# Row products and convolution taps from GpSimd and ScalarE to VectorE, and another start for a ring of split weights

## The chip, the cores and the metric

The kernel runs on one core of a Trainium2 chip. The metric is the device time in microseconds (us) of one execution, and lower is better. The core's engines run side by side: TensorE (PE in the rows) multiplies matrices, VectorE (DVE), ScalarE (ACT) and GpSimd (POOL) work on elements, SyncE (SP) issues most transfers. Each engine takes its instructions in the order in which they stand in its queue.

## What is computed

Two transformer blocks of two layers each, one after the other, in f32 on 512 positions of 1024 features. The change lies in the second block and at the seam to it. Of the reference, this is what the changed lines compute:

```python
return rmsnorm(x, final_norm_w)                    # end of the first block
...
for l in range(DEPTH):                             # second block
    h = rmsnorm_2(x, norm_mix_g[l]) * (1.0 + sc1) + sh1
    u = h @ w_in[l]
    ...                                            # four mixers on slices of u
    y_conv = conformer_conv(cu, conv_w[l], conv_b[l], conv_ln_g[l], conv_ln_b[l])
    mix = jnp.concatenate([y_fox, y_pool, y_ret, y_conv], axis=-1)
    x = x + g1 * (mix @ w_out[l])
    h = rmsnorm_2(x, norm_ffn_g[l]) * (1.0 + sc2) + sh2
    f = (jax.nn.silu(h @ ffn_w1[l]) * (h @ ffn_w3[l])) @ ffn_w2[l]
    x = x + g2 * f

def conformer_conv(u, conv_w, conv_b, ln_g, ln_b):
    a, gate = jnp.split(u, 2, axis=-1)
    h = a * jax.nn.sigmoid(gate)
    h = lax.conv_general_dilated(                  # 31 taps, one filter per channel
        h, conv_w[:, None, :], window_strides=(1,), padding=[(CONV_WIDTH - 1, 0)],
        dimension_numbers=('NWC', 'WIO', 'NWC'), feature_group_count=CONV_CH) + conv_b
    return jax.nn.silu(layernorm(h, ln_g, ln_b))
```

The convolution has 256 channels, which are two tiles of 128 channels x 512 positions.

## The kernel before

Features lie on the 128 partitions, positions along the free axis: x is eight tiles of 128x512. Every f32 product of matrices is made of three products of rounded parts: `mm3` (L290 to L292) multiplies the high part of a weight with the high part of the input, the same with the input's low part, and the weight's low part with the input's high part. Inputs are split into `hx[0]` (high) and `hx[1]` (low) by `modulate`: a product `hmod` on VectorE (L522), the high part on ScalarE (L523) and the low part on VectorE (L524), in halves of 256 positions.

The class `Weights` loads each weight into one of four `wraw` buffers and splits it: `whi` by a copy on ScalarE (L204), `wlo = wraw - whi` by a subtraction on VectorE (L205), for a few entries of the plan on GpSimd in two halves. `parts` says where the two results lie. In the mixers that is the pool `split`, with two buffers. While `extra` is set, which is so in the feed-forward, a pool of its own with two more pairs joins, and `n_ring` alternates between the two, beginning with `extra`. The memory of `extra` was the mixers' before, and becomes free as the mixers end.

At the end of the first block, `w_out_phase` with l = 1 makes the last norm twice: into `hx`, from which the second block's mixers start, and into the tiles `x2`, which carry x on. `Norm.rows` turns a column of 512 factors into `R1`, a 128x512 tile in PSUM with the same row on all partitions, ScalarE copies it to SBUF (`R1s`), and GpSimd multiplies the eight tiles of `x2` with it (L724).

In the mixers (class `Mix`) the projection `w_in` goes through TensorE slice by slice, while the parts of the mixers that are ready run beside it. `conv_in` makes, for each of its two tiles, the gated input `hp` and hands a generator of 31 taps to a list from which a few are drawn after each weight. A tap adds 512 columns of `hp`, shifted by one more, times a column of `cw`, to the sum `cacc`. For tile 0 every tap is one instruction on VectorE (L2105). For tile 1, taps 1 to 30 are two: ScalarE makes the product `tap` (L2108), GpSimd adds it (L2109). `conv_out` then sums over both tiles on GpSimd (`both`, L2138) and normalises.

The order of the instructions on each engine comes from a scheduler that places them by its own estimate of their times; `issue_after` is a hint to it that one is to come behind another. So an edit in one place moves instructions in others too.

In the feed-forward, weights 0 and 2 are from w1, 1 and 3 from w3 for the first two slices, which are made with `mm3` into `dps`. After them a scheme with fewer products follows: it needs eight sums of `hx` parts (`xa`, L1496), four more (L1499 to L1505), and the matmuls into `sd`, `sfc`, `sy` and others (L1522 to L1524).

Of the kernel before, what the change touches and what calls it, by code (L numbers as in the profile page):

```python
# [9 lines left out]
F32 = mybir.dt.float32  # L10
# [3 lines left out]
AF = mybir.ActivationFunctionType  # L14
OP = mybir.AluOpType
# [24 lines left out]
KORD = (4, 5, 6, 7, 8, 9, 10, 11, 0, 1, 2, 3)  # L40
LEAD = (0.22, 0.35)
MLEAD = 0.45
PTAP = (0, 31)
CONVW = 2
OORD = (2, 0, 3, 6, 7, 4, 5, 1)
TRATE = (3, 3)
# [10 lines left out]
def parts(x, bits):  # L57

    out = []
    for _ in range(3):  # L60
        e = math.floor(math.log2(abs(x)))
        c = math.floor(x / 2.0 ** (e - bits + 1)) * 2.0 ** (e - bits + 1)
        out.append(c)
        x -= c
    return out + [x]


TURN = parts(2 * math.pi, 9)
PI_LO = 3.1415925

# [5 lines left out]
class Weights:  # L76
# [45 lines left out]

    def parts(self):

        self.n_ring = (self.n_ring + 1) % 2 if self.extra else 0
        pool, k = (self.extra, {"bufs": 2}) if self.n_ring else (self.split, {})
        return [pool.tile([128, KD * 128], F32R, tag=x, name=x, **k) for x in ("whi", "wlo")]

    def free(self, n):
# [153 lines left out]
class Kern:  # L283
# [340 lines left out]
    def w_out_phase(self, l, s):  # L624
        tc, nc, a = self.tc, self.nc, self.a
        V, A = nc.vector, nc.scalar
# [20 lines left out]
        m = self.mod[l]  # L647
        acc = xp.tile([128, 512], F32, name="accx")
        acc2 = xp.tile([128, 512], F32, name="accc")
        if l:  # L650
            x2, fw = self.B2.x, self.vecs[:, 64:72]
# [33 lines left out]
        for ct in range(7):  # L685
            px = self.pt("d", "wox")
            pc = self.pt("pt" if ct else "d", "woc") if l == 0 else None
            for p in range(2):
                w = self.W.next()
# [6 lines left out]
        w = [self.W.next(2 - i) for i in range(2)]  # L696
# [21 lines left out]
        if l:  # L718
            R1 = self.pt("pt", "R1")
            nm.rows(R1, 0, 4, 2, 0)  # L720
            R1s = self.tmp.tile([128, 512], F32, tag="hmod", name="R1s")
            A.activation(R1s, R1, AF.Copy)
            for k in range(8):
                nc.gpsimd.tensor_tensor(x2[:, k, :], x2[:, k, :], R1s, op=OP.mult)  # L724


class Attn:
# [921 lines left out]
class Mix:  # L1649
# [442 lines left out]
    def conv_in(self, t):  # L2092
        nc = self.nc
        V, A, tc = nc.vector, nc.scalar, self.K.tc
        hp, acc = self.hp[t], self.cacc[t]

        def taps():
            for i in range(31):
                src, w = hp[:, 2 + i:514 + i], self.cw[:, t, i:i + 1]
                s, v = self.K.W.last  # L2100
                with tc.issue_after(s), tc.issue_after(v):
                    if i == 0:
                        V.tensor_scalar(acc, src, w, self.col(2, t), op0=OP.mult, op1=OP.add)
                    elif i >= PTAP[t]:
                        V.scalar_tensor_tensor(acc, src, w, acc, op0=OP.mult, op1=OP.add)  # L2105
                    else:
                        m = self.K.tmp.tile([128, 512], F32, tag="hmod", name="tap")
                        A.activation(m, src, AF.Copy, scale=w)  # L2108
                        nc.gpsimd.tensor_tensor(acc, acc, m, op=OP.add)  # L2109
                yield  # L2110

        def f(ps):
            nc.gpsimd.memset(hp[:, 0:32], 0.0)
            nc.vector.scalar_tensor_tensor(hp[:, 32:], self.th, 1.0, ps, op0=OP.add, op1=OP.mult)
            self.taps.append((taps(), TRATE[t]))
        return f
# [305 lines left out]
```

## Time and profile before

| | |
|---|---|
| median of three runs | 2502.6 us (2501.32 to 2503.1) |
| the profiled execution | 2502.77 us, span 2501.0 us |
| busy: TensorE, VectorE | 2359.8 us (94%), 1922.1 us (77%) |
| busy: ScalarE, GpSimd | 1365.9 us (55%), 222.2 us (9%) |
| first mixers and their feed-forward entry | from 1282 to 1552 us of the span |
| second mixers and their feed-forward entry | from 1895 to 2162 us of the span |

Times in the rows are microseconds from the start of the span. A row of a timeline is one instruction or several alike that follow each other: start, busy time, engine, line, operation, what is written and read, the count, and in brackets how long the engine sat idle before and what ended that. Instructions of one engine overlap a little, so a row's time is more than its distance to the next. In the rows the tile x2 is called x, and R1 is R. Lines are those of the kernel before; in the changed kernel the same lines stand one to seven lower.

### The profile page before, as it was taken

The page shows a single profiled execution, that of the slowest core. Times are in us where ns is not written, and L with a number is a line of the kernel's source. Part 1 is how long each engine was busy: PE and PEld are TensorE (multiplying, and loading weights), DVE is VectorE, ACT ScalarE, POOL GpSimd, SP SyncE. Part 2 cuts the span into 40 slices and gives each one's busy share as a digit, 9 for nine tenths or more (in the row PEclk, how much of TensorE's full clock was granted, in tenths as well). Part 3 has the DMA queues.
Part 4 walks back from the last instruction along what each step waited for, and adds up shares of the span by engine and source line. Part 5 has one row for each costly group of instructions (what it writes and reads, how often), then busy time and mean ns, then how long its engine had stood idle before and what let it go on. Part 6 is the DMA issues. An engine that isn't in the chain of part 4 may idle for free. (4 is left out here: it accounts for less than half of the span.)

```text
span 2501.0 us, 37762 instructions
## 1 busy us (share of the span) xinstructions
PE 2359.8 (94%) x14392; PEld 2034.3 (81%) x14392; DVE 1922.1 (77%) x3269; ACT 1365.9 (55%) x2656; POOL 222.2 (9%) x206
## 2 busy tenths in 40 slices
PE   7899999999998999999987998999999899899998
PEld 3788888888887788888775778989897578899897
DVE  5778777888356888888579868999767985967675
ACT  4566555668345654578546555535355655545453
POOL 0110000000020000000035201000002510100000
PEclk9999999999999999999989999999999899999999
DMA  6113323223331146532422122676332212242422
GB/s 258 48 55 93 97 95 103 88 85 125 131 96 50 45 150 217 190 120 64 133 73 65 54 66 78 232 247 213 116 101 76 66 56 68 85 132 72 128 71 72
DMA packets 87749, 269.67 MB, mean 108 GB/s; under 512 B 12048, under 2 KB 22544, under 8 KB 87184
## 3 DMA queue, kind: packets, MB, share of 16 engines
q1 hardware_dynamic: 78240, 232.79, 28.9%
q10 hardware_dynamic: 6912, 25.17, 2.9%
q0 software_dynamic: 2416, 9.31, 1.0%
q8 instruction: 113, 1.85, 0.3%
q14 instruction: 68, 0.56, 0.1%
HBM read 255.82 MB, written 11.40 MB: 107 GB/s over the span
## 5 line engine op out<-in xcount | busy, mean ns | idle before, releaser
L290 PE MATMUL dps<-hx,whi 128*128 128x512 f32 (+1 forms) x1040 | 417.0, 401 | 16.1 <-ACT q L1747 5.0
L292 PE MATMUL dps<-hx,wlo 128*128 128x512 f32 (+1 forms) x1040 | 404.4, 389 | 9.4 <-DVE wlo L205 8.3
L291 PE MATMUL dps<-hx,whi 128*128 128x512 f32 (+1 forms) x1040 | 405.2, 390 | 2.8 <-DVE hx L524 1.7
L204 ACT ACTIVATE whi<-wraw 128x1024 fp32r<-128x1024 f32 (+2 forms) x202 | 194.0, 964 | 263.6 <-issue 84.3
L205 DVE TENSOR_TENSOR wlo<-wraw,whi 128x1024 fp32r<-128x1024 f32 (+1 forms) x182 | 221.8, 1219 | 82.0 <-ACT whi L204 80.4
L290 PEld LDWEIGHTS dps<-hx,whi 128*128 128x128 f32 x1040 | 203.4, 196 | 46.1 <-DVE t L1770 6.4
L292 PEld LDWEIGHTS dps<-hx,wlo 128*128 128x128 f32 x1040 | 203.0, 195 | 46.1 <-DVE wlo L205 9.1
L1165 ACT ACTIVATE ph<-PT 128x512 fp32r<-128x512 f32 (+1 forms) x280 | 152.9, 559 | 135.7 <-PE PT L1160 132.4
L291 PEld LDWEIGHTS dps<-hx,whi 128*128 128x128 f32 x1040 | 203.3, 195 | 27.6 <-DVE hx L524 3.3
L1166 DVE TENSOR_TENSOR pl<-PT,ph 128x512 fp32r<-128x512 f32 (+1 forms) x280 | 175.3, 642 | 44.6 <-ACT ph L1165 42.4
L162 ACT ACTIVATE whi<-wraw 128x512 fp32r<-128x512 f32 x200 | 119.5, 625 | 131.7 <-PE spt L1523 42.4
L1148 PE MATMUL Y<-ph,vt 128*128 128x256 f32 (+1 forms) x592 | 161.1, 282 | 6.6 <-ACT ph L1165 2.8
L1160 PE MATMUL PT<-ident,P 128*128 128x128 f32 x1024 | 160.0, 276 | 5.9 <-DVE pl L1166 4.0
L1149 PE MATMUL Y<-pl,vt 128*128 128x256 f32 (+1 forms) x592 | 162.5, 290 | 2.7 <-DVE pl L1166 2.6
L290 PE MATMUL w2p<-g,whi 128*128 128x512 f32 (+1 forms) x364 | 140.5, 386 | 0.0
L291 PE MATMUL w2p<-g,whi 128*128 128x512 f32 (+1 forms) x364 | 140.4, 386 | 0.0
L292 PE MATMUL w2p<-g,wlo 128*128 128x512 f32 (+1 forms) x364 | 140.4, 386 | 0.0
L1160 PEld LDWEIGHTS PT<-ident,P 128*128 128x128 f32 x1024 | 118.8, 141 | 23.2 <-DVE pl L1166 9.7
L1148 PEld LDWEIGHTS Y<-ph,vt 128*128 128x128 f32 x592 | 111.6, 189 | 28.2 <-ACT ph L1165 19.0
L1099 PE MATMUL S<-kt,qt 128*128 128x256 f32 (+2 forms) x576 | 126.7, 328 | 1.7 <-DVE nm L1117 0.9
L1149 PEld LDWEIGHTS Y<-pl,vt 128*128 128x128 f32 x592 | 111.8, 189 | 13.7 <-DVE pl L1166 6.1
L1118 ACT ACTIVATE P<-P,nm 128x512 f32<-128x512 f32 (+1 forms) x128 | 94.9, 742 | 47.5 <-DVE nm L1117 46.0
(477 smaller groups left out, 6546.2 us busy)
## 6 DMA issues: line engine op xcount, KB each, us to landing
wraw<-ffn_w SPq DMA_DIRECT2D x120, 512.0 KB, 4.4
wraw<-w_in SPq DMA_DIRECT2D x112, 512.0 KB, 3.5
adaw<-ada_wt SPq DMA_DIRECT2D x80, 512.0 KB, 4.0
adab<-ada_wt ACTq DMA_DIRECT2D x48, 512.0 KB, 5.2
wraw<-w_out SPq DMA_DIRECT2D x32, 384.0 KB, 3.1
aw<-ada_w SPq DMA_DIRECT2D x16, 512.0 KB, 10.2
wraw<-w_out SPq DMA_DIRECT2D x16, 512.0 KB, 3.5
bias<-bias_b SPq DMA_DIRECT2D x16, 384.0 KB, 3.7
```

Source lines behind the costliest of these rows:

```text
L162: self.nc.scalar.activation(hi[:, j * w:j * w + w], x, AF.Copy)
L204: s = self.nc.scalar.activation(hi[:, q], t[:, q], AF.Copy)
L205: v = E.tensor_tensor(lo[:, q], t[:, q], fr(hi[:, q]), op=OP.subtract)
L290: mm(ps, hi, xh, start=start, stop=False)
L291: mm(ps, hi, xl, start=False, stop=False)
L292: self.mm_last = mm(ps, lo, xh, start=False, stop=stop).ins
L1099: mm(S[:, so:so + n], Q[:, j, qc], Kt[:, i, ko:ko + n], start=i == 0, stop=i == 1)
L1148: mm(o, v, ph[:, co:co + w], start=b == 0 and n == 0, stop=False, skip_group_check=True)
L1149: mm(o, v, pl[:, co:co + w], start=False, stop=b == len(banks) - 1 and n == len(items) - 1, skip_group_check=True)
L1160: nc.tensor.transpose(pst[:, col:col + 128], ps[t][:, pc:pc + 128], K.ident)
L1165: A.activation(ph[:, :col], pst[:, :col], AF.Copy)
L1166: V.tensor_tensor(pl[:, :col], pst[:, :col], fr(ph[:, :col]), op=OP.subtract)
```

## The change

Three edits. In `w_out_phase`, VectorE multiplies the eight tiles of `x2` with `R1` in PSUM, and ScalarE's copy goes. In `conv_in`, all taps of both tiles are one instruction on VectorE; 30 taps per layer move. In `Weights.parts`, the ring of the feed-forward counts four and takes the pool `split` for the first two pairs and `extra` for the next two, where it took them in turn.

```diff
-PTAP = (0, 31)
...
     def parts(self):
 
-        self.n_ring = (self.n_ring + 1) % 2 if self.extra else 0
-        pool, k = (self.extra, {"bufs": 2}) if self.n_ring else (self.split, {})
+        pool, k = (self.extra, {"bufs": 2}) if self.extra and self.n_ring > 1 else (self.split, {})
+        self.n_ring = (self.n_ring + 1) % 4 if self.extra else 0
         return [pool.tile([128, KD * 128], F32R, tag=x, name=x, **k) for x in ("whi", "wlo")]
...
             R1 = self.pt("pt", "R1")
             nm.rows(R1, 0, 4, 2, 0)
-            R1s = self.tmp.tile([128, 512], F32, tag="hmod", name="R1s")
-            A.activation(R1s, R1, AF.Copy)
             for k in range(8):
-                nc.gpsimd.tensor_tensor(x2[:, k, :], x2[:, k, :], R1s, op=OP.mult)
+                V.tensor_tensor(x2[:, k, :], x2[:, k, :], R1, op=OP.mult)
...
                     if i == 0:
                         V.tensor_scalar(acc, src, w, self.col(2, t), op0=OP.mult, op1=OP.add)
-                    elif i >= PTAP[t]:
+                    else:
                         V.scalar_tensor_tensor(acc, src, w, acc, op0=OP.mult, op1=OP.add)
-                    else:
-                        m = self.K.tmp.tile([128, 512], F32, tag="hmod", name="tap")
-                        A.activation(m, src, AF.Copy, scale=w)
-                        nc.gpsimd.tensor_tensor(acc, acc, m, op=OP.add)
```

VectorE's queue at the start of the first mixer, before (hx_79 is the low part of the input, ck a constant of the mixers, cw the filters):

```order
L524 SCALAR_TENSOR_TENSOR hx_79<-hmod,mod_9634,hx_78 128x256 x2
L522 TENSOR_TENSOR hmod<-x,rrow 128x256 x2
L1845 CAST ck<-ones 64x512
L524 SCALAR_TENSOR_TENSOR hx_79<-hmod,mod_9634,hx_78 128x256 x2
L205 TENSOR_TENSOR wlo<-wraw,whi 128x1024
L1664 TENSOR_SCALAR cw<-cw 128x62
L205 TENSOR_TENSOR wlo<-wraw,whi 128x1024
L2114 SCALAR_TENSOR_TENSOR hp_13601<-th,dps 128x512
```

The same place of VectorE's queue after the change (x_12850 is x2, R_13556 is R1):

```order
L521 TENSOR_TENSOR hmod<-x,rrow 128x256 x2
L721 TENSOR_TENSOR x_12850<-x_12850,R_13556 128x512
L523 SCALAR_TENSOR_TENSOR hx_79<-hmod,mod_9634,hx_78 128x256 x2
L521 TENSOR_TENSOR hmod<-x,rrow 128x256 x2
L721 TENSOR_TENSOR x_12850<-x_12850,R_13556 128x512
L523 SCALAR_TENSOR_TENSOR hx_79<-hmod,mod_9634,hx_78 128x256 x2
L721 TENSOR_TENSOR x_12850<-x_12850,R_13556 128x512 x3
L1661 TENSOR_SCALAR cw<-cw 128x62
L204 TENSOR_TENSOR wlo<-wraw,whi 128x1024
L1842 CAST ck<-ones 64x512
L204 TENSOR_TENSOR wlo<-wraw,whi 128x1024
```

Five of the eight products stand between the pairs that make hx, three behind the last pair and ahead of the first split; `cw` moved ahead of the split and `ck` behind it.

VectorE's queue in the convolution of the first mixer, before (cacc_13603 is the sum of tile 0; ql and k are parts of attention):

```order
L2105 SCALAR_TENSOR_TENSOR cacc_13603<-hp_13601,cw,cacc_13603 128x512 x2
L1770 TENSOR_TENSOR t_13903<-dps,ct_12851 128x512
L1774 TENSOR_TENSOR t_13904<-t_13904,st_12852 128x512
L2105 SCALAR_TENSOR_TENSOR cacc_13603<-hp_13601,cw,cacc_13603 128x512
L1775 TENSOR_TENSOR t_13903<-t_13903,t_13904 128x512
L208 SCALAR_TENSOR_TENSOR wlo<-wraw,whi 128x1024
L1754 TENSOR_TENSOR k<-t_13903,k 64x512 x2
```

The same place after the change (cacc_13601 is the sum of tile 0, cacc_13602 that of tile 1):

```order
L1767 TENSOR_TENSOR t_13893<-dps,ct_12851 128x512
L2102 SCALAR_TENSOR_TENSOR cacc_13602<-hp_13600,cw,cacc_13602 128x512
L1771 TENSOR_TENSOR t_13894<-t_13894,st_12852 128x512
L2102 SCALAR_TENSOR_TENSOR cacc_13601<-hp_13599,cw,cacc_13601 128x512
L1772 TENSOR_TENSOR t_13893<-t_13893,t_13894 128x512
L2102 SCALAR_TENSOR_TENSOR cacc_13602<-hp_13600,cw,cacc_13602 128x512
L2102 SCALAR_TENSOR_TENSOR cacc_13601<-hp_13599,cw,cacc_13601 128x512
L1751 TENSOR_TENSOR k<-t_13893,k 64x512 x2
L2102 SCALAR_TENSOR_TENSOR cacc_13602<-hp_13600,cw,cacc_13602 128x512
L207 SCALAR_TENSOR_TENSOR wlo<-wraw,whi 128x1024
```

Taps of tile 1 stand between those of tile 0 and the other mixers' work.

TensorE's queue at the entry of layer 1's feed-forward, before (ssum and rrow are the norm, dps with 512 positions the feed-forward's first products):

```order
L292 MATMUL wo_15438<-mix_13585,wlo 128x256
L250 MATMUL ssum<-ones,acc 128x1
L250 MATMUL ssum<-ones,sql 128x1
L250 MATMUL ssum<-ones,acc 128x1
L250 MATMUL ssum<-ones,sql 128x1
L267 MATMUL rrow<-ident,rstd 128x128 x2
L290 MATMUL dps<-hx_78,whi 128x512
L291 MATMUL dps<-hx_79,whi 128x512
L292 MATMUL dps<-hx_78,wlo 128x512
```

The same place after the change:

```order
L291 MATMUL wo_15376<-mix_13583,wlo 128x256
L249 MATMUL ssum<-ones,acc 128x1
L289 MATMUL dps<-hx_78,whi 128x256
L290 MATMUL dps<-hx_79,whi 128x256
L291 MATMUL dps<-hx_78,wlo 128x256
L289 MATMUL dps<-hx_78,whi 128x256
L290 MATMUL dps<-hx_79,whi 128x256
```

The products of the first 256 positions moved ahead of the rest of the norm. Further on in the same queue, after the change, where weights 2 and 3 begin:

```order
L289 MATMUL dps<-hx_78,whi 128x512
L290 MATMUL dps<-hx_79,whi 128x512
L1519 MATMUL sd<-hx_78,whi 128x256
L1520 MATMUL sd<-hx_79,whi 128x256
L1519 MATMUL sfc<-hx_78,whi 128x256
L1520 MATMUL sfc<-hx_79,whi 128x256
L1519 MATMUL sy<-hx_78,whi 128x256
L1520 MATMUL sy<-hx_79,whi 128x256
L291 MATMUL dps<-hx_78,wlo 128x512
```

Six matmuls of the part that follows moved ahead of the first product that reads a `wlo` of weight 2 or 3. On VectorE that `wlo` stands behind the sums; after the change:

```order
L523 SCALAR_TENSOR_TENSOR hx_79<-hmod,mod_9634,hx_78 128x256 x2
L1493 TENSOR_TENSOR xa<-hx_78,hx_79 128x512 x4
L139 TENSOR_TENSOR wsum<-wsum,wraw 128x512
L1493 TENSOR_TENSOR xa<-hx_78,hx_79 128x512 x4
L1496 TENSOR_TENSOR xa<-xa 128x4x256
L204 TENSOR_TENSOR wlo<-wraw,whi 128x1024
L1498 TENSOR_TENSOR xa<-xa 128x4x256
L204 TENSOR_TENSOR wlo<-wraw,whi 128x1024
```

Before, the first of these two stood in the same place, and the second among the last pairs of hx.

## Rows read from the trace of the kernel before

**Rows 1.** The page's busy times, share of span, instructions.

```profile
PE 2359.8 (94%) x14392; PEld 2034.3 (81%) x14392; DVE 1922.1 (77%) x3269; ACT 1365.9 (55%) x2656; POOL 222.2 (9%) x206
```

**Rows 2.** Stretches: length, busy PE, PEld, DVE, ACT, POOL, granted clock, DMA, GB/s.

```profile
1275.00:1291.30 16.30, 7.96 (x65) 7.53 (x64) 14.12 (x13) 7.06 (x10) 12.25 (x14) 0.81 0.09 21
...
1304.70:1412.00 107.30, 89.06 (x362) 67.22 (x361) 98.18 (x134) 62.83 (x98) 51.13 (x36) 0.90 0.21 63
1412.00:1518.90 106.90, 103.09 (x558) 84.91 (x556) 77.44 (x147) 59.84 (x118) 8.76 (x10) 1.00 0.19 60
1518.90:1552.60 33.70, 27.46 (x152) 23.92 (x153) 31.79 (x51) 17.44 (x29) 5.41 (x4) 0.85 0.30 94
```

**Rows 3.** Timeline of GpSimd at the first mixer's start.

```profile
1280.27 9.88 POOL L724 TENSOR_TENSOR x<-x,R1s 128x512 f32<-128x512 f32 x8
```

**Rows 4.** Timeline of VectorE there.

```profile
1276.14 0.89 DVE L524 SCALAR_TENSOR_TENSOR hx<-hmod,mod,hx 128x256 fp32r<-128x256 f32 x2 [0.24 <-ACT hx L523]
...
1278.07 0.86 DVE L524 SCALAR_TENSOR_TENSOR hx<-hmod,mod,hx 128x256 fp32r<-128x256 f32 x2
1280.84 10.39 DVE L205 TENSOR_TENSOR wlo<-wraw,whi 128x1024 fp32r<-128x1024 f32 x1 [1.90 <-ACT whi L204]
...
1291.26 1.21 DVE L205 TENSOR_TENSOR wlo<-wraw,whi 128x1024 fp32r<-128x1024 f32 x1
```

**Rows 5.** Timeline of TensorE there, and one matmul in the convolution.

```profile
1282.20 0.28 PE L292 MATMUL dps<-hx,wlo 128*128 128x256 f32 x1
...
1291.29 0.80 PE L292 MATMUL dps<-hx,wlo 128*128 128x512 f32 x1 [8.35 <-DVE wlo L205]
...
1296.46 0.39 PE L292 MATMUL dps<-hx,wlo 128*128 128x512 f32 x1
...
1391.68 0.64 PE L290 MATMUL dps<-hx,whi 128*128 128x512 f32 x1 [1.77 <-ACT q L1747]
```

**Rows 6.** VectorE's instructions by line, 1304.7 to 1412: count, busy, mean ns.

```profile
L2105 DVE SCALAR_TENSOR_TENSOR cacc<-hp,cw,cacc 128x512 f32<-128x512 f32 x26 | 28.3, 1089 | 0.2
...
L1770 DVE TENSOR_TENSOR t<-dps,ct 128x512 f32<-128x512 f32 x4 | 2.8, 692 | 0.1
```

**Rows 7.** Timeline of VectorE in the convolution of layer 1.

```profile
1300.99 2.33 DVE L2105 SCALAR_TENSOR_TENSOR cacc<-hp,cw,cacc 128x512 f32<-128x512 f32 x3
...
1307.71 2.45 DVE L2105 SCALAR_TENSOR_TENSOR cacc<-hp,cw,cacc 128x512 f32<-128x512 f32 x2
...
1339.78 0.74 DVE L2105 SCALAR_TENSOR_TENSOR cacc<-hp,cw,cacc 128x512 f32<-128x512 f32 x1
1340.44 0.68 DVE L1775 TENSOR_TENSOR t<-t,t 128x512 f32<-128x512 f32 x1
...
1404.58 1.54 DVE L1850 COPY cumhi<-ck 32x512 f32<-32x512 f32 x1
```

**Rows 8.** Instructions that write tile tap: ns, least, median, most.

```profile
L2108 ACT ACTIVATE tap<-hp,cw x60: 706/717/732, 1305.5 to 2010.9; 128x512 f32<-128x512 f32 x60
```

**Rows 9.** Waits of 1304.7 to 1412: total us, times, longest.

```profile
PE tps L1760 <- ACT ft L1788: 4.2, 2, 2.7
```

**Rows 10.** Timeline of TensorE at the entry of layer 1's feed-forward.

```profile
1521.85 0.59 PE L250 MATMUL ssum<-ones,sql 128*128 128x1 f32 x2 [2.96 <-ACT sql L1419]
...
1525.22 0.69 PE L267 MATMUL rrow<-ident,rstd 128*128 128x128 f32 x2 [1.94 <-POOL rstd L260]
...
1552.63 0.28 PE L1522 MATMUL sd<-hx,whi 128*128 128x256 f32 x1
```

**Rows 11.** Timeline of GpSimd there.

```profile
1516.65 2.88 POOL L205 TENSOR_TENSOR wlo<-wraw,whi 128x512 fp32r<-128x512 f32 x2 [2.49 <-ACT whi L204]
...
1533.29 3.17 POOL L205 TENSOR_TENSOR wlo<-wraw,whi 128x512 fp32r<-128x512 f32 x2 [8.12 <-ACT whi L204]
```

**Rows 12.** Timeline of VectorE there.

```profile
1533.51 4.71 DVE L1496 TENSOR_TENSOR xa<-hx,hx 128x512 f32<-128x512 f32 x4
...
1542.28 1.22 DVE L205 TENSOR_TENSOR wlo<-wraw,whi 128x1024 fp32r<-128x1024 f32 x1
```

## The prediction

> **What bounds the kernel now.** I read the line of busy times first: TensorE is busy 94% of the span, VectorE 77%, ScalarE 55%, GpSimd 9% [rows 1]. So a change on VectorE and GpSimd pays only where TensorE waits. The table by stretches shows where [rows 2]. At the start of the first mixer (1275 to 1291.3) TensorE is busy 7.96 of 16.3 us. In the stretch in which the convolution runs (1304.7 to 1412 in layer 1, and one like it in layer 2) it is busy 89.06 of 107.3 us and VectorE 98.18: there VectorE sets the pace. From 1412 to 1518.9 TensorE is busy 103.09 of 106.9, so that stretch is TensorE's. At the entry of the feed-forward (1518.9 to 1552.6) both are short of time: 27.46 and 31.79 of 33.7 us. The change acts at the start of mixer 1, in the two convolution stretches and at the two entries, five places, and the rest of the span should keep its time. The execution that was profiled took 2502.77 us (span 2501.0); the median of the three runs is 2502.6, and the sum is made against 2502.77.
>
> **Part 1, the row products (once).** GpSimd multiplies eight 128x512 tiles in 9.88 us [rows 3]. VectorE's split `wlo` at L205 starts at 1280.84 in the same moment and takes 10.39 us, where the next one of the same form takes 1.21 [rows 4]: both engines read two SBUF operands, and VectorE's instruction ends only when GpSimd's eight are through. TensorE waits for that split for 8.35 us, and the matmuls of 128x512 behind it are slow: the first that is back at 0.39 us is the one at 1296.46 [rows 5]. The granted clock is 0.81 in this stretch [rows 2], so TensorE runs at the lower of its two levels for a while, 1.2 instead of 2.4 GHz. The twelve matmuls from 1291.29 take 5.2 us where twelve at full pitch (0.234) take 2.8: with the first one's longer start left out, 2.2 us.
>
> With the change VectorE does the eight products, reading R1 in PSUM. The nearest row is the 128x512 product with a PSUM operand at L1770: 0.69 us [rows 6], and as the next instruction of VectorE starts some 0.09 us before one ends (the tap at 1339.78 and the row after it [rows 7]), 0.60 of it counts. Five stand between the pairs that make hx and three behind them. Four of the five fill a wait of 0.24 us for ScalarE in which VectorE idled [rows 4]: hx is ready 5 x 0.60 - 4 x 0.24 = 2.0 us later, at 1278.93 + 2.0, about 1281.0 (the first also waits for R1's transposes, and the CAST of `ck` goes behind the split; I let the two cancel). TensorE's products with this half of hx end at 1282.3 and move by about as much less 0.2, to 1284.1; two more matmuls (0.47) come before the split is needed. Three more products (1.8), `cw` (0.1) and the split (1.2) end at 1281.0 + 3.1 = 1284.1. So TensorE goes on at about 1284.6 instead of 1291.3: 6.7 us. How much of the 2.2 us of clock comes back is open. TensorE will still wait nearly 2 us for hx, and a wait of 1.77 us in front of 1391.68 was followed by nine matmuls like the 0.64 there [rows 5], 1.7 us. I credit the difference, 0.5, which makes **7.2 us**. Bounds: 4, when each product delays hx by its full length and TensorE's later wait takes part of the gain, and 6.7 + 2.2 = 8.9. ScalarE loses a copy of 0.60 us there, which was beside other work; I count it at nothing.
>
> **Part 2, 30 taps of tile 1 (each mixer).** A tap on VectorE takes 0.75 us undisturbed (1339.78), and the next instruction starts 0.66 later; three that depend on each other take 2.33 us, 0.78 each (1300.99) [rows 7]. In the new order taps of the two tiles alternate, so I take 0.66: 30 x 0.66 = 19.8 us more on VectorE per mixer. What goes is the disturbance. Two taps beside GpSimd's first adds take 2.45 us (1307.71), about 1.0 more than two alone [rows 7]. Over the stretch the 26 taps have a mean of 1089 ns, 26 x 0.34 = 8.8 us more than at 0.75, while the PSUM form at L1770 stays at 692 [rows 6]. Splits, rope products and small rows are hit as well: row by row 26 instructions, from the taps at 1307.71 to the COPY of 1.54 us at 1404.58, are longer than their like by 23.5 us in all [rows 7], and layer 2 has as many. Net, VectorE has 23.5 - 19.8 = 3.7 us less per mixer. ScalarE loses 30 x 0.717 = 21.5 us (`tap` at L2108) [rows 8]. VectorE's idle time in the stretch is 107.3 - 98.2 = 9.1 us, waits for ScalarE and TensorE in the main, and TensorE waits there for ScalarE's `ft` for 4.2 us [rows 9]: a freer ScalarE can shorten both a little. I take **4.0 us per mixer**, 8.0 in all. Bounds per mixer: 0, if taps run at the 0.78 of dependent ones (30 x 0.78 = 23.4), and 3.7 + 4.2 = 7.9, if the wait for `ft` goes as well. What comes after 1412 is TensorE's stretch, and it hides nothing of this: it just starts earlier. GpSimd's sum `both`, which waited for the last add, has then its two operands from VectorE.
>
> **Part 3, the ring (each entry).** Now TensorE idles at the entry for 2.96 and 1.94 us [rows 10], and the granted clock of the stretch is 0.85 [rows 2]. Weight 0 of the feed-forward waits there for memory of the mixers: its two halves are split on GpSimd at 1533.29, behind a wait of 8.12 us, those of weight 1 already at 1516.65 [rows 11]. After the change weights 0 and 1 both lie in the old pool, and both are split before hx is ready, so the new order puts weight 0's and 1's products for the first half into the idle time. Weights 2 and 3 then both lie in the extra pool, and their `wlo` come on VectorE only behind the eight sums `xa` and two more instructions. Now one such stands there, at 1542.28; the one of weight 3 is done ahead. The sums will lose GpSimd's disturbance (four take 4.71 us from 1533.51, and at a pitch of 0.60 it would be 2.5), so VectorE could come to the first `wlo` up to 2 us earlier; I count on one and place it at 1541 [rows 12]. hx is ready just when those sums begin, at 1533.5; TensorE is through with weights 0 and 1 near 1534.5 and has ten matmuls, 1.6 us, before it needs that `wlo`: a new wait of about 5 us. From there weights 2 and 3 take 44 matmuls x 0.234 = 10.3 us, to 1551.3. Now the next part starts at 1552.63 [rows 10], and six of its matmuls (0.7 us) will be done: 2.0 us gained, of which a clock that falls in the new wait takes about as much (nine matmuls, 1.7 us, as above). I take **0** per entry. Bounds: a loss of 3.5, if the wait is followed by a half clock as long as the one at 1291 and the extra GpSimd splits at 1519 to 1522 hold up hx as well (two at 1.0 us), and a gain of 3, if the clock stays.
>
> **Sum.** 7.2 + 2 x 4.0 + 2 x 0 = 15.2 us: 2502.77 - 15.2 = **2487.5 us**.
>
> **Rivals.**
> (a) The entries pay too. For it: the idle time of 4.9 us [rows 10] is of the kind that the ring moves work into, and with it the clock would fall less. If the `wlo` of weights 2 and 3 come when TensorE asks, each entry gives some 5.5 us: 2476.5. Against it: in the new order they stand behind eight sums.
> (b) VectorE is the bound and more work there costs. It is 92% busy in the convolution [rows 2], and the gain hangs on the whole 23.5 us of disturbance coming back. If only a fraction f does, each mixer loses 19.8 - 23.5 f: the taps alone break even at f = 0.84, and the whole change is slower by over 5 us from f = 0.58 down. At f = 0.5 the two mixers cost 16.1 us against part 1's 7.2: 2511.7. For it: the 0.66 is read from few undisturbed rows, and VectorE's later instructions may inherit other waits. Against it: the long rows stand where an add of GpSimd runs and 0.74 us rows right beside them [rows 7], and one split lost as much as eight of GpSimd's products took [rows 3, 4], so I give it little. The Trainium skill (Perfetto Trace Analysis, Optimizing Scalar/DVE Operations) says that work of a saturated VectorE may well be given to ScalarE or even GpSimd, against which this change goes; the same paragraph adds that VectorE and GpSimd share a read port, so that moving work between those two might not help. The 10.39 us of the split agree with the second half [rows 4]; whether more work on a busy VectorE costs more than it frees, no row of before shows.
> (c) No change. The entries lose 3.5 us each with a fallen clock, and the mixers gain nothing, since taps at 0.78 eat the disturbance: 7.2 - 7.0 leaves 2502.6.
> (d) Only part 1 shows: the waits for ScalarE and TensorE bind VectorE in the mixers, and the entries are even: 2495.5.
>
> **How the numbers follow.** A difference under 0.2%, 5.0 us, can't be told from none in this kernel. Chances: the forecast (2480 to 2494) 0.52, (a) 0.15, (d) 0.13, (c) 0.11, (b) 0.09. Faster: 0.52 + 0.15 + 0.13 = 0.80; same 0.11; slower 0.09. The bounds of the parts add to a gain between -3 and 31 us, but not all at once; a range of 2475 to 2500 leaves out (b), the far part of (a) and half of (c), about 0.2.
>
> **What would show it.** Part 1: the split at the start of mixer 1 takes 1.2 us and TensorE's wait for it of 8.35 us is gone, with a shorter one for hx in its place. Part 2: 120 taps at 0.75 us, no 128x512 instruction of VectorE over 1 us in the mixers, VectorE busy about 94.5 us where it had 98.2, and that stretch about 4 us shorter. Part 3: no waits for `sql` and `rstd`, one of about 5 us for a `wlo` at L205, and the next part (L1522) as long after the end of `wo` as now, 33.7 us. I am wrong if the long rows stay without GpSimd's adds, if the convolution stretch keeps its length with VectorE less busy, or if the entries move by more than 3 us either way.

## The result, and the profile after

The changed kernel takes 2479.9 us (median of four runs, 2478.9 to 2483.9) against 2502.8: a ratio of 0.991, 95% interval 0.990 to 0.993. In a later series of runs it took 2480.4 us against 2508.4 of the kernel before on the same chip (0.988, interval 0.987 to 0.990). So the gain is 22.9 us, and in the second series 28: the kernel before scatters more (2500 to 2515 us) than the changed one. The forecast was 2487.5 us in a range of 2475 to 2500: right in sign and range, but 7.7 us short of the gain. The profiled execution of after took 2483.9 us, the slowest of its four; it began its second block 3 us later than the one of before, so stretches are compared by their own length, not by their place.

The first line is the page's line of busy times after, to be read against [rows 1]; below it stretches of after, answering to [rows 2]: length, then busy PE, PEld, DVE, ACT and POOL, granted clock, DMA share, GB/s.

```profile
PE 2354.0 (95%) x14392; PEld 2028.6 (82%) x14392; DVE 1902.7 (77%) x3337; ACT 1326.0 (53%) x2595; POOL 113.0 (5%) x138
...
1297.90:1397.00 99.10, 84.76 (x366) 63.61 (x364) 94.21 (x165) 43.70 (x69) 2.41 (x6) 0.97 0.21 68
1397.00:1503.70 106.70, 102.37 (x551) 84.30 (x551) 75.26 (x146) 59.11 (x116) 8.22 (x10) 1.00 0.20 60
1503.70:1537.00 33.30, 27.70 (x157) 23.30 (x156) 29.84 (x50) 19.05 (x33) 4.97 (x4) 0.90 0.29 95
```

TensorE has the same 14392 matmuls, and the 6 us that it is busy less go with the granted clock, whose mean over the span is 0.978 before and 0.983 after. The convolution stretch fell from 107.3 to 99.1 us with VectorE busy 94.2 of it, where the prediction had 94.5. The stretch behind it and the feed-forward's entry kept their lengths.

At the start of the first mixer, VectorE's timeline of after, which answers to [rows 3, 4]:

```profile
1273.62 0.69 DVE L721 TENSOR_TENSOR x<-x,R 128x512 f32<-128x512 f32 x1 [0.99 <-PE R L266]
...
1282.43 0.87 DVE L523 SCALAR_TENSOR_TENSOR hx<-hmod,mod,hx 128x256 fp32r<-128x256 f32 x2
1283.22 1.87 DVE L721 TENSOR_TENSOR x<-x,R 128x512 f32<-128x512 f32 x3
1285.02 0.18 DVE L1661 TENSOR_SCALAR cw<-cw 128x62 f32<-128x62 f32 x1
1285.12 1.22 DVE L204 TENSOR_TENSOR wlo<-wraw,whi 128x1024 fp32r<-128x1024 f32 x1
```

and TensorE's timeline there, which answers to [rows 5]:

```profile
1282.18 0.38 PE L289 MATMUL dps<-hx,whi 128*128 128x256 f32 x1 [0.33 <-ACT hx L522]
1282.96 0.38 PE L290 MATMUL dps<-hx,whi 128*128 128x256 f32 x1 [0.40 <-DVE hx L523]
...
1286.88 0.39 PE L291 MATMUL dps<-hx,wlo 128*128 128x512 f32 x1
```

and the stretch around it, up to the second `hp` (columns as above):

```profile
1278.00:1297.89 19.89, 19.16 (x114) 16.55 (x114) 15.28 (x28) 8.74 (x14) 2.21 (x6) 1.00 0.40 122
```

The split is back at 1.22 us, and TensorE reads it at 1286.88 without a wait, at 0.39 us: two waits of 0.33 and 0.40 us stand where one of 8.35 stood, and the granted clock stays at 1.00.

The taps of after, by the tile's view (ns: least, median, most), beside [rows 6, 7]:

```profile
L2102 DVE SCALAR_TENSOR_TENSOR cacc<-hp,cw,cacc x120: 732/746/755, 1290.9 to 2001.9; 128x512 f32<-128x512 f32 x120
```

Not one of the 120 taps is longer than 0.755 us, where one in the kernel before reached 1.79, and from the first split to the end of `wo` in both mixers no 128x512 instruction of VectorE takes 0.9 us.

For the rest of the text the trace is cut at marks that both kernels have. Each number is the length in us between the starts of two instructions in the profiled execution of that kernel. `cvr` is the row of means of the convolution's layernorm, which TensorE makes once the sums of all taps are finished; `wo` is the mixers' output, and its end is its last matmul; `hs` are the split sums of the feed-forward's input, and `w2p` its output.

| from, to | before | after | after again | rows alone | taps alone | ring alone | rows and taps |
|---|---|---|---|---|---|---|---|
| last transpose of R1, second hp of mixer 1 | 34.6 | 24.7 | 24.7 | 24.8 | 35.0 | 34.6 | 24.8 |
| second hp, first cvr, layer 1 | 110.1 | 101.9 | 103.3 | 109.5 | 103.7 | 110.1 | 103.1 |
| the same, layer 2 | 112.2 | 103.7 | 102.6 | 112.1 | 102.7 | 112.7 | 101.7 |
| end of wo, first sd from hs, layer 1 | 40.4 | 39.6 | 41.2 | 40.0 | 40.4 | 39.7 | 40.5 |
| from there to the first w2p, layer 1 | 54.2 | 56.2 | 56.1 | 54.2 | 54.9 | 54.7 | 54.2 |
| from there to the last w2p, layer 1 | 268.6 | 274.2 | 272.4 | 268.1 | 269.2 | 269.7 | 270.4 |
| end of wo, last w2p, layer 2 | 361.2 | 358.8 | 359.4 | 360.6 | 359.8 | 359.2 | 360.1 |

### The profile page after: what moved, and what is told of

Same layout as the page of the kernel before. It is cut to its first block, busy times and chain, and to the rows that moved or that the text cites. A ratio compares the mean times of both kernels' runs of the same rounds, so it can differ in the third digit from the quotient of the medians.

```text
span 2482.1 us, 37640 instructions
## 1 busy us (share of the span) xinstructions
PE 2354.0 (95%) x14392; PEld 2028.6 (82%) x14392; DVE 1902.7 (77%) x3337; ACT 1326.0 (53%) x2595; POOL 113.0 (5%) x138
## 5 line engine op out<-in xcount | busy, mean ns | idle before, releaser
L289 PE MATMUL dps<-hx,whi 128*128 128x512 f32 (+1 forms) x1040 | 412.7, 398 | 22.1 <-ACT q L1744 8.1
L290 PE MATMUL dps<-hx,whi 128*128 128x512 f32 (+1 forms) x1040 | 401.0, 387 | 5.7 <-DVE hx L523 4.4
L203 ACT ACTIVATE whi<-wraw 128x1024 fp32r<-128x1024 f32 (+2 forms) x202 | 194.1, 964 | 272.6 <-issue 93.6
L204 DVE TENSOR_TENSOR wlo<-wraw,whi 128x1024 fp32r<-128x1024 f32 (+1 forms) x182 | 209.3, 1151 | 75.9 <-ACT whi L203 74.5
L289 PEld LDWEIGHTS dps<-hx,whi 128*128 128x128 f32 x1040 | 200.9, 193 | 51.3 <-ACT q L1744 8.9
L290 PEld LDWEIGHTS dps<-hx,whi 128*128 128x128 f32 x1040 | 200.5, 193 | 31.5 <-DVE hx L523 7.1
L1163 DVE TENSOR_TENSOR pl<-PT,ph 128x512 fp32r<-128x512 f32 (+1 forms) x280 | 175.2, 641 | 43.4 <-ACT ph L1162 41.2
L1145 PEld LDWEIGHTS Y<-ph,vt 128*128 128x128 f32 x592 | 112.2, 190 | 28.5 <-ACT ph L1162 19.5
## 6 DMA issues: line engine op xcount, KB each, us to landing
aw<-ada_w SPq DMA_DIRECT2D x16, 512.0 KB, 10.2
```

The costliest lines, as they stand in the source:

```text
L203: s = self.nc.scalar.activation(hi[:, q], t[:, q], AF.Copy)
L204: v = E.tensor_tensor(lo[:, q], t[:, q], fr(hi[:, q]), op=OP.subtract)
L289: mm(ps, hi, xh, start=start, stop=False)
L290: mm(ps, hi, xl, start=False, stop=False)
L1145: mm(o, v, ph[:, co:co + w], start=b == 0 and n == 0, stop=False, skip_group_check=True)
L1163: V.tensor_tensor(pl[:, :col], pst[:, :col], fr(ph[:, :col]), op=OP.subtract)
```

## The experiments

**One part alone, and two.** Four kernels in one series, each the kernel before with some of the three edits; e4 has the edits of e1 and e2.

```diff
e1_rows
-            R1s = self.tmp.tile([128, 512], F32, tag="hmod", name="R1s")
-            A.activation(R1s, R1, AF.Copy)
             for k in range(8):
-                nc.gpsimd.tensor_tensor(x2[:, k, :], x2[:, k, :], R1s, op=OP.mult)
+                V.tensor_tensor(x2[:, k, :], x2[:, k, :], R1, op=OP.mult)
e2_taps
-PTAP = (0, 31)
+PTAP = (0, 0)
e3_ring
-        self.n_ring = (self.n_ring + 1) % 2 if self.extra else 0
-        pool, k = (self.extra, {"bufs": 2}) if self.n_ring else (self.split, {})
+        pool, k = (self.extra, {"bufs": 2}) if self.extra and self.n_ring > 1 else (self.split, {})
+        self.n_ring = (self.n_ring + 1) % 4 if self.extra else 0
```

> The kernel before with the row products alone moved to VectorE; taps and ring as before. The traces of before and after differ by 9.9 us between the last transpose of R1 and the second hp of mixer 1. If that is the row products' own, the time is near 2493 us (ratio 0.996). By the prediction's sum it was 7.2 us: 2495.6. If part of it came from the taps or the ring, less than 5 us.

Measured: 2494.3 us against 2504.9 (ratio 0.995, interval 0.993 to 0.996), 10.6 us. The table has 9.9 us of it between the last transpose of R1 and the second hp, and the convolution stretches keep their 109.5 and 112.1. The interval alone doesn't tell 9.9 from 7.2 us; by the trace the row products are worth 10 us by themselves, not 7.2.

> The kernel before with the 30 taps of tile 1 per layer alone moved to VectorE. By the traces the convolution stretch, from the second hp to the first cvr, shrinks by 8.1 us in layer 1 and 8.4 in layer 2: near 2486 us (0.993). By the prediction's sum, 4.0 per mixer: 2494.8. If VectorE's load counted alone, 3.7 per mixer.

Measured: 2489.7 us (0.993, interval 0.991 to 0.996), 15.1 us. The two convolution stretches are 6.4 and 9.4 us shorter, 15.8 together, so about 8 per mixer and twice the forecast.

> The kernel before with the new ring alone. Prediction: 0 per entry, so 2502.8 within 3 us, with a new wait for wlo of 2 to 5 us at L205 in place of those for sql and rstd. Rival: the early products pay, 5 us per entry, near 2493. Second rival: the feed-forward of layer 1, 6.7 us longer in the one profile of after, is longer because of the ring: 2505 or more.

Measured: 2511.2 us, the median of ten runs from 2503 to 2514; the kernel before had a median of 2504.9 beside it and runs from 2500 to 2514, and the ratio is 1.001, interval 1.000 to 1.003. The waits changed as foretold (none for `sql` and `rstd`, one of 2.2 us for a `wlo`), but the ring is no gain: it lies between nothing and a loss of 7 us.

> The changed kernel with the old ring. If the ring is worth nothing, the same as the changed kernel, 2480 within 3 us. If the ring pays at the entries, slower than 2483; if it costs in layer 1, about 2475.

Measured: 2476.9 us (2475.1 to 2479.5; 0.989, interval 0.986 to 0.991), 28.0 us less than the kernel before beside it. Rows alone and taps alone give 10.6 + 15.1 = 25.7, so the two add up within the scatter, and the changed kernel, which has the ring besides, is no faster than without it: 2479.9 and 2480.4 us, 0.991 and 0.988 of the kernel before beside each, in other series.

**Whose time comes back in the convolution.** By [rows 8] ScalarE is freed of 21.5 us per mixer by the same edit that takes the adds off GpSimd. This kernel frees VectorE of GpSimd and leaves ScalarE its load. The edit, on the changed kernel:

```diff
+PTAP = (0, 31)
...
+                    elif i >= PTAP[t]:
+                        V.scalar_tensor_tensor(acc, src, w, acc, op0=OP.mult, op1=OP.add)
                     else:
-                        V.scalar_tensor_tensor(acc, src, w, acc, op0=OP.mult, op1=OP.add)
+                        m = self.K.tmp.tile([128, 512], F32, tag="hmod", name="tap")
+                        A.activation(m, src, AF.Copy, scale=w)
+                        V.tensor_tensor(acc, acc, m, op=OP.add)
```

> The changed kernel, but a tap of tile 1 stays in two parts: ScalarE makes the product as before, VectorE (not GpSimd) adds it. So GpSimd's adds are gone, VectorE has as many instructions as in the changed kernel, and ScalarE keeps its 21.5 us per mixer. Theory A (half of the 8.2 us per mixer is VectorE's lost disturbance, the other half the freed ScalarE): a convolution stretch of about 106 us from the second hp to the first cvr, against 102 after and 110 before, and 2488 in all. Rival B (it is all VectorE's and GpSimd's port): 102 us as after, 2480. Rival C (it is all ScalarE's): 110, 2496.

Measured: 2479.6 us, beside 2480.4 of the changed kernel in the same series. The convolution stretches, by the view of stretches (columns as above): first this kernel,

```profile
1294.86:1398.14 103.28, 92.19 (x392) 69.95 (x390) 95.83 (x171) 65.59 (x103) 4.65 (x6) 0.94 0.23 70
1903.61:2006.25 102.64, 91.25 (x391) 69.10 (x390) 94.86 (x170) 66.04 (x102) 4.57 (x6) 0.95 0.23 70
```

then the changed kernel in the same series,

```profile
1295.09:1398.42 103.33, 89.74 (x379) 67.33 (x377) 95.72 (x169) 44.94 (x71) 3.77 (x6) 0.93 0.21 65
1902.08:2004.70 102.62, 88.43 (x379) 66.40 (x377) 95.72 (x169) 46.24 (x72) 3.77 (x6) 0.95 0.22 65
```

and the kernel before:

```profile
1304.67:1414.74 110.07, 91.61 (x376) 69.12 (x374) 100.22 (x139) 63.51 (x99) 51.83 (x36) 0.91 0.20 61
1911.97:2024.12 112.15, 93.64 (x377) 70.57 (x375) 101.39 (x141) 64.84 (x100) 51.75 (x36) 0.89 0.19 60
```

ScalarE has 65.6 us of work in the first pair, as before, and 44.9 in the second, and the lengths agree to 0.05 us. So theory A, which I held when I wrote it, falls: the freed ScalarE gave nothing, and all 8 us per mixer are the adds taken off GpSimd. ScalarE's waits for the buffer of `tap` aren't the cause either: they are 11.2 us in ten places of the kernel before, over both mixers, where an add of GpSimd has to release it, and 15.8 us in fourteen places of e5, where one of VectorE does.

**How far VectorE sets the pace there.** One kernel leaves work out, one moves it. First:

```diff
-            for i in range(31):
+            for i in range(31 if t == 0 else 1):
```

> The changed kernel with taps 1 to 30 of tile 1 left out in both layers (that part of the convolution is not computed), which takes 19.8 us of VectorE's 94.2 from each convolution stretch. If VectorE alone sets the pace there, the stretch falls from 102 to 82 us; TensorE was busy 84.8 us in it, so it can't. Theory: it falls until TensorE's work is the bound, to about 90, 12 us less per mixer, 2456 in all. Rival: waits between engines set the pace as much as VectorE's load, and only 4 us go per mixer: 2472.

Measured: 2450.2 us, 30.2 less than the changed kernel beside it. Its convolution stretch in layer 1, by the same view:

```profile
1296.51:1383.08 86.57, 82.10 (x378) 63.63 (x376) 76.87 (x138) 43.62 (x70) 3.81 (x6) 1.00 0.26 77
```

VectorE lost 18.9 us (95.7 to 76.9) and the stretch 16.8 (103.3 to 86.6), 16.2 in layer 2: nearly nine tenths of each microsecond taken from VectorE come off the end, until TensorE, now at full clock, is busy 82.1 of 86.6. The theory's 12 us per mixer was the nearer of the two answers and still 4 too little. Its 90 us had TensorE at its old 84.8 us of work, counted up to a little before cvr; the clock gave some of that back.

```diff
e8_swap_act
-    def swap_halves(self, dst, src):
+    def swap_halves(self, dst, src, swd=SWD):
...
-                if a < SWD:
+                if a < swd:
...
-            K.swap_halves(t2, ps)
+            K.swap_halves(t2, ps, 0)
```

> The changed kernel with the mixers' COPY of 32x512 at L501, four per layer, moved from VectorE to ScalarE, which has room (43.7 of 99.1 us). If VectorE sets the pace in the convolution, it loses 4 x 0.61 = 2.4 us per mixer and the whole is 4.9 us faster, about 2475. If the order of VectorE and ScalarE in the rope chain sets it, nothing or a loss of 1 per mixer, 2482.

Measured: 2474.2 us (0.986, interval 0.984 to 0.988), 6.2 less than the changed kernel, which is the first of the two answers. VectorE is busy 92.9 us in the stretch, 2.8 less, and the stretches are 100.1 and 100.7 us, 3.2 and 1.9 less. It is faster than the changed kernel beside it, clear of the scatter. The Trainium skill (Perfetto Trace Analysis, Optimizing Scalar/DVE Operations) names both moves: work of a saturated VectorE may go to ScalarE or GpSimd, and between VectorE and GpSimd it might not help because of a shared port. Both halves hold here: eight copies to ScalarE gave 6 us, and sixty adds taken back from GpSimd gave 15.

> The changed kernel once more, beside the others of this call. Its profile before had 274.2 us between the first and the last w2p of layer 1 against 268.6 in the kernel before. If that is scatter of the loads, here 268 to 271 and the gain over the kernel before is 23 to 26 us; if it belongs to the new ring, again 274.

Measured: 2480.4 us, and 272.4 us between those marks. Neither of the two answers: it is above 271 and below 274, and the gain of 28.0 us is above the 23 to 26.

**What the row products still cost.**

```diff
             for k in range(8):
-                V.tensor_tensor(x2[:, k, :], x2[:, k, :], R1, op=OP.mult)
+            V.tensor_tensor(x2[:, 0, :], x2[:, 0, :], R1, op=OP.mult)
```

> The changed kernel with seven of the eight row products left out (those tiles of x2 are not scaled). It shows what the products still cost where they stand now. In the trace of after TensorE waits 0.33 and 0.40 us for hx there and for nothing else, so at most about 1 us goes: 2479. By the prediction's working, which had VectorE's seven products of 0.60 on the path of hx and of the first split, 2 to 3 us go: 2477.

Measured: the place is 0.9 us shorter (from the last transpose of R1 to the first hp 15.5 us, against 16.4), near the 0.7 us of the trace's two waits and not the 2 to 3 us of the prediction's working. The whole took 2481.9 us, in the scatter of the changed kernel.

**The ring, with the copies on ScalarE.** e9 has the old ring, e8_again the new one, e10 begins with split and takes turns. All else is the same.

```diff
e10_ring_turned, against the old ring
-        self.n_ring = (self.n_ring + 1) % 2 if self.extra else 0
-        pool, k = (self.extra, {"bufs": 2}) if self.n_ring else (self.split, {})
+        pool, k = (self.extra, {"bufs": 2}) if self.extra and self.n_ring else (self.split, {})
+        self.n_ring = (self.n_ring + 1) % 2 if self.extra else 0
```

> The kernel with the copies on ScalarE (as e8_swap_act) and the old ring. In the profiles the new ring left the two entries as they were and made layer 1's feed-forward longer behind them, by 1.9 us to the first w2p and 2 to 3 us up to the last. Theory: the old ring is worth 3 to 4 us, this one is faster than e8_again beside it by that, near 2471. Rival: that was scatter of the loads, and the two are the same.

> e8_swap_act once more, beside e9 and e10, which differ from it by the ring alone: 2474 again.

> As e8_again, but the ring takes split and extra in turn and begins with split (weights 0 and 2 in split, 1 and 3 in extra). If the loss in layer 1 comes from the first sums for the second layer's modulation being placed behind weights 2 and 3, it is the same here, where VectorE's order has them as late (the first 83 places behind the sums xa, in the old ring 58): 2474. If it comes from weights 2 and 3 both lying in extra, this one is as fast as e9, 2471.

Measured: e9 2470.7 us (0.987, interval 0.985 to 0.989), e8_again 2472.9 (0.988, 0.987 to 0.989), e10 2473.7 (0.988, 0.987 to 0.990). The old ring is ahead by 2.2 us, but the intervals overlap. From the first sd out of hs to the first w2p of layer 1 the three take 54.2, 56.0 and 54.4 us, from there to the last w2p 270.3, 270.1 and 273.1. So the 1.9 us in the first of these stretches belong to the new ring (55.7 to 56.2 in the seven profiles that have it beside the moved taps, 54.7 in e3, 54.2 in four of the five with the old one and 54.9 in e2), but the second scatters from run to run by as much as the ring would explain. Of the kernels that leave nothing out e9 is the fastest, 31.9 us below the kernel before and some 9 below the changed one in other series, of which 6 are the copies.

## Why the prediction was right, and where it fell short

**What bounds the kernel** held. The time went where TensorE had waited, and the stretches that were called TensorE's kept their length: from the first cvr to the end of wo 103.8 us before and 103.9 after.

**Part 1** was forecast at 7.2 and measured 9.9, both in after and in e1. Two terms were mis-sized. TensorE's start at the split moved by 7.5 us against R1's last transpose (21.25 us before, 13.72 after), where the working had 6.7: the last hx came 1.25 us later, not 2.0. The term for the clock was the larger: I expected a wait of nearly 2 us for hx and credited 0.5 of the 2.2 us that the slow matmuls cost. The waits were 0.33 and 0.40 us, the matmuls behind them are at 0.39 us, and the whole 2.2 came back. e7 agrees that no more than 0.9 us was left in this place.

**Part 2** was forecast at 4.0 per mixer, with bounds of 0 and 7.9, and measured 8.1 and 8.4 in after, just past the upper bound, and 6.4 and 9.4 in e2. The stretches of after, second hp to first cvr in layers 1 and 2, to be read beside those of the kernel before under e5:

```profile
1297.89:1399.82 101.93, 87.38 (x379) 65.56 (x378) 95.64 (x169) 45.08 (x71) 3.78 (x6) 0.97 0.20 66
1903.57:2007.28 103.71, 89.72 (x380) 67.82 (x378) 95.72 (x169) 46.24 (x72) 3.78 (x6) 0.93 0.21 65
```

The 0.66 us a tap and the disturbance were right to within 2 us, and VectorE's load of 94.5 us was close. The step that failed is the one that followed them: it took the difference in VectorE's load (3.7; by the rows 100.2 - 95.6 = 4.6 in layer 1 and 101.4 - 95.7 = 5.7 in layer 2) for nearly the whole gain, kept the 9.1 us in which VectorE idled (9.9 between these marks), and looked to ScalarE for the rest. These are VectorE's longest waits in the stretch of layer 1, first before,

```profile
DVE mix L2079 <- ACT mix L2078: 2.0, 1, 2.0
DVE ql L300 <- ACT q L299: 2.0, 1, 2.0
DVE ret L2019 <- POOL rst L2017: 1.8, 1, 1.8
DVE hp L2114 <- PE dps L292: 1.3, 1, 1.3
DVE cumhi L1850 <- ACT cq L1849: 1.2, 1, 1.2
```

then after (total us, times, longest):

```profile
DVE ret L2016 <- POOL rst L2014: 2.1, 1, 2.1
DVE hp L2107 <- PE dps L291: 1.4, 1, 1.4
DVE ph L299 <- ACT ph L298: 1.0, 2, 0.6
DVE t L1767 <- ACT t L503: 0.9, 2, 0.5
DVE k L1751 <- ACT k L1750: 0.5, 1, 0.5
```

The idle time fell with the disturbance, from 9.9 to 6.3 us. Most of it was named after ScalarE, but e5 has ScalarE as loaded as before, and its stretch is as short. What else moved is TensorE's clock: in the kernel before the granted clock was at its lower level for 20.5 us of this stretch in layer 1 and 24.7 in layer 2 (means 0.91 and 0.89 in the rows), in after for 6.8 and 13.7 (0.97 and 0.93), and TensorE's busy time fell from 91.6 to 87.4 and from 93.6 to 89.7 with the same matmuls. A VectorE that is held up makes TensorE wait, TensorE then runs slower for a while, and VectorE waits in turn for what ScalarE makes of TensorE's sums (`ql` and `cumhi` in the rows). How much that is worth can be estimated from the profiles that have all taps on VectorE and a load of 95.6 to 95.7 us on it (after, after again, e2, e4, e7; two stretches each): where the clock was at its lower level for 6.8 us the stretch took 101.7 to 101.9 us, for 10.2 us 102.6 to 103.1, and for 13.7 us 103.3 to 103.7. That is 1.8 us for 6.9 us of clock. The 13.7 us of clock that layer 1 got back between before and after are then 3.5 us, and the 11.0 of layer 2 are 2.8; what the load leaves open is 8.1 - 4.6 = 3.5 and 8.4 - 5.7 = 2.7. So the estimate closes the sum. It doesn't tell whether the clock or the waits come first, and that one follows from the other is argued, not shown, since no kernel held the clock up and left the adds in place.

**Part 3** was forecast at 0 per entry, and the entries did stay: by the table from 40.4 to 39.6 and 41.2 us in layer 1, and between the same marks from 39.8 to 39.7 and 39.4 in layer 2. (In layer 1 the two profiles of the changed kernel differ by the clock, which is at its lower level for 6.8 us of the entry in the first and for 13.7 in the second.) The new wait came, in TensorE's timeline of after, to be read beside [rows 10]:

```profile
1506.65 0.39 PE L290 MATMUL dps<-hx,whi 128*128 128x256 f32 x1 [0.79 <-DVE hx L523]
...
1522.04 0.38 PE L1519 MATMUL sd<-hx,whi 128*128 128x256 f32 x1 [1.47 <-ACT whi L161]
1523.60 0.50 PE L1519 MATMUL sy<-hx,whi 128*128 128x256 f32 x1 [0.53 <-ACT whi L161]
1526.31 0.80 PE L291 MATMUL dps<-hx,wlo 128*128 128x512 f32 x1 [2.00 <-DVE wlo L204]
```

TensorE waits 0.79, 1.47, 0.53 and 2.00 us, 4.8 in all, and 0.7 in two shorter waits; the matmul behind the last takes 0.80 us, and the granted clock is 0.50 from 1523.7 to 1530.5. That is the size of the 4.9 us that went [rows 10], beside which three shorter waits of 1.6 us stood. The wait for `wlo` itself is 2.0 and not 5, since TensorE comes to it later: it waits for hx and for two `whi` of ScalarE first, which the working didn't have. VectorE and GpSimd there, which answer to [rows 11, 12]:

```profile
1502.00 5.74 POOL L204 TENSOR_TENSOR wlo<-wraw,whi 128x512 fp32r<-128x512 f32 x4 [2.49 <-ACT whi L203]
```

```profile
1503.67 2.92 DVE L523 SCALAR_TENSOR_TENSOR hx<-hmod,mod,hx 128x256 fp32r<-128x256 f32 x2
...
1518.48 2.49 DVE L1493 TENSOR_TENSOR xa<-hx,hx 128x512 f32<-128x512 f32 x4
...
1525.04 1.22 DVE L204 TENSOR_TENSOR wlo<-wraw,whi 128x1024 fp32r<-128x1024 f32 x1
```

The four splits on GpSimd make one pair of hx take 2.92 us where an undisturbed one takes 0.87, as the bound had it, and the sums run undisturbed. The first `wlo` starts 21.3 us after the end of wo, the working had 22.5.

What part 3 missed lies outside the five places: "the rest of the span should keep its time". Layer 1's feed-forward behind the entry got 1.5 to 1.9 us longer up to the first w2p in every kernel that has the ring with the moved taps, and 1.4 to 5.7 longer from there to the last w2p, where the old ring beside moved rows or taps had -0.5 to 1.8. In the first part TensorE has no wait at all in the kernel before, e1, e4 and e9; in after it waits 1.1 and 0.3 us for `up`, which VectorE makes of the feed-forward's products. TensorE's longest wait in the latter part, before and after, is for `up` too:

```profile
PE sfa L1522 <- DVE up L1612: 2.1, 1, 2.1
```

```profile
PE sfa L1519 <- DVE up L1609: 4.8, 1, 4.8
```

In the order of VectorE's instructions the sums for the second layer's modulation begin 85 places behind the first `xa` with the new ring and 58 with the old one (instructions alike that follow each other count as one place), and layer 2, which has no such sums, lost nothing (361.2 to 358.8). That points to them, but e10, with sums as late (83), lost almost nothing in the first part (54.4) and as much in the second (273.1), so the cause of the 3 us or so stays open, and so does their size: alone the ring's ratio is 1.000 to 1.003, and e8_again and e9 overlap.

**The sum.** By the runs: rows 10.6, taps 15.1, ring -3 by 2480 against e4's 2476.9: 22.7, and 22.9 were measured. That the two agree so well is partly luck, since the -3 compares different series: by the ratio to the kernel before beside each, the changed kernel's 0.991 and 0.988 lie on both sides of e4's 0.989. The forecast had 7.2, 8.0 and 0. That it was off by no more than 7.7 us is luck in part as well, as both gains were larger and a cost stood against them which it didn't have. Of the rivals, (b) was wrong by its own test, since all of the disturbance came back, and (d) and (c) fell with it. (a) gave nearly the right time, 2476.5, for a reason that is wrong: the entries paid nothing.

## What to carry to other kernels

Where an engine sets the pace of a stretch, price what you take off it at its full length and count its waits with it: waits that are named after another engine may go as well, here 8.1 us where the load alone said 4.6, and e6's slope of 0.89 was to be had from one kernel with work left out. GpSimd's help was not free here while VectorE worked on SBUF operands: the pair of rows to look for is one instruction of VectorE longer than its like and one of GpSimd beside it. An edit of the order can be paid for outside the place that it was made for, as the 1.5 to 1.9 us behind the entry show, so lay out the whole span by marks before you call a part even.

## What the runs showed of the hardware

VectorE's split lost more than one instruction of GpSimd: it began 0.57 us behind the first of eight products that follow each other at 1.24 us and ended only when all were through, 10.39 us instead of 1.21 [rows 3, 4]. Single adds with gaps between them cost a VectorE instruction that works on SBUF alone up to 1.1 us each, 0.9 as the mean of the prediction's 26. In the rows that loss is the rest of the add that is under way when the instruction starts, less 0.1 to 0.2 us: a tap at 1308.50 loses 0.92 with 1.12 left, the product at 1315.55 (L1774) 0.39 with 0.52 left, a split at 1311.10 0.09 with 0.22 left. It isn't limited to two operands: the COPY of 32x512 at L1850 takes 1.54 us beside an add and 0.42 without one. Instructions with one operand in PSUM show none of it. Four of the eight at L1770 lie wholly within an add and take 0.69 us like the rest, here with the long instruction that follows:

```profile
1337.67 1.64 POOL L2109 TENSOR_TENSOR cacc<-cacc,tap 128x512 f32<-128x512 f32 x1 [0.59 <-ACT tap L2108]
```

```profile
1338.19 0.69 DVE L1770 TENSOR_TENSOR t<-dps,ct 128x512 f32<-128x512 f32 x1
1338.80 1.06 DVE L1774 TENSOR_TENSOR t<-t,st 128x512 f32<-128x512 f32 x1
```

Executions of one kernel scatter by as much as a small effect: the kernel before had medians of 2502.6 to 2508.4 us in four series on several chips, and ten runs of e3 in one series lay between 2503 and 2514. Effects under 3 us, the ring's among them, could not be settled by the runs made.
